# Nine of eleven feed-forward pairs as seven block products instead of seven, with normed operands from the second pair on

## The chip, the core and the metric

The kernel runs on one core of a Trainium2 chip. The core has engines with a queue each: TensorE for matmuls (PE in the profile; PEld is its weight load), VectorE (DVE), ScalarE (ACT), GpSimd (POOL) and SyncE (SP), which here only issues DMAs. On-chip data lies in 128 partitions; matmuls write to accumulators in PSUM, which VectorE and ScalarE read. The metric is the device time of one execution in microseconds (us); lower is better. Before the change the median of three runs is 1290.93 us.

## The reference

Two decoder layers on 512 tokens of width 1024 in float32. Each layer ends in a SwiGLU feed-forward and a gated embedding; only the feed-forward is touched:

```python
def rms_norm(x, g):
    xf = x.astype(jnp.float32)
    y = xf * lax.rsqrt(jnp.mean(xf * xf, axis=-1, keepdims=True) + EPS)
    return (y * g.astype(jnp.float32)).astype(x.dtype)

def swiglu(x, w_gate, w_up, w_down):
    return (jax.nn.silu(x @ w_gate) * (x @ w_up)) @ w_down
...
        u = rms_norm(h, ffn_norm_g[i])
        h = h + swiglu(u, ffn_w_gate[i], ffn_w_up[i], ffn_w_down[i])
```

The inner width is 2816, that is 22 blocks of 128.

## The kernel before

**Arithmetic.** Activations are kept transposed: a chunk is 128 features x 512 tokens, and the width of 1024 is eight chunks. Each float32 operand is split into an upper part (rounded by ScalarE) and the remainder (by VectorE). `mm3` (lines 161 to 165) makes one product of three matmuls, in this order: weight remainder by upper activation (163), upper weight by activation remainder (164), upper by upper (165).

**Feed-forward** (`ffn`, called once in each layer). The 22 blocks are taken two at a time, as eleven pairs, in three parts of 4, 4 and 3 pairs; after each part `linear` multiplies the hidden blocks by the down weights and adds them to `h`. `after.chunk` prepares the next norm.

A *direct* pair takes four weight tiles (gate and up of each block; `weight`, lines 146 to 159: a DMA on SyncE's queue into `wraw`, the upper part `whi` at 156, the remainder `wlo` at 158) and for each weight eight products with the chunks: 4 x 8 x 3 = 96 matmuls of 512 columns. The rows are `mm` in the profile.

The first pairs of a feed-forward (`RAW_PAIRS`) read raw chunks (`norm.u`, tiles `A`), which are not yet divided by the root mean square; the result is multiplied by the row `rb` (lines 745 and 747). `rb` is made from column sums (line 203), a diagonal matrix (227), a spreading matmul (237) and a copy by ScalarE (212). `normed` is a generator that `feed` advances: for each of the eight chunks it makes the normed chunk (592; tiles of the tags in `qtags`, and `wth` for the last two), its upper part (598) and its remainder (599), which later direct pairs read (`un`). After `uses[0] = None` it goes on to eight more steps: it makes differences of blocks of 256 columns of the normed chunks (618) and splits them (621, 622) into tiles `A`. `STEPS` says how many steps follow each half of a pair.

A pair *as seven products* (`strassen`) takes the gate weights of both blocks as a matrix of 2 x 2 blocks, and the up weights likewise, and forms each result from seven block products in place of eight, 7 x 4 x 3 = 84 matmuls of 256 columns each time. `operands` makes the combined weights: a tile of a tag in `qtags`, in the profile `C`, is loaded on SyncE's queue (649) and a second weight is added to it by an accumulating DMA on GpSimd's queue (650); a raw weight goes into `wraw` (652); sums with it are `wth` (666) and `wtl` (667); `split` makes upper parts and remainders (642, 643) in the ring of four `whi` and four `wlo`. The order of the products is 1 (which needs only `wraw`), 5 and 7 (the combined tile `C`), 2 and 6, 4, 3.

The tags of `SPACE` have two buffers at most, and the normed chunks lie in the same tags as the combined weights: in the first feed-forward chunks 0 to 3 in two buffers of `C5` and 4, 5 in `C4`; in the second 0, 1 in `C2`, 2, 3 in `C3` and 4, 5 in `C4`. The three tags are used in turn, beginning with the second of `qtags`.

**Order.** Each engine takes its queue in order. The program is written as above; a scheduler sets the order in each queue ahead of time, from its own model of times.

Before, the first two pairs of each feed-forward read raw chunks, the third and fourth normed ones, and the seven pairs of parts two and three are made of products.

Of the kernel before, what the change touches and what calls it, by code (L numbers as in the profile page):

```python
# [23 lines left out]
NC = D // P  # L24
# [57 lines left out]
    (("C5", "C5", "C4"), [(f"C{k // 2}",) for k in range(8)]),  # L82
    (("C2", "C3", "C4"), [(t,) for t in ("C0", "C0", "C1", "C1", "C5", "C5")] + [("D0", "D1"), ("D4", "D5")]),
)
RAW_PAIRS = 2
STEPS = (0, 2, 3, 3)
SEVEN = ((1,0),(1,1),(1,2),(1,3),(2,0),(2,1),(2,2))
QKV = (("q", 0, (0, 0, 0, 0)), ("v", 0, (0, 1, 1, 0)), ("q", 1, (1, 1, 2, 2)), ("q", 2, (0, 1, 2, 0)), ("v", 1, (1, 2, 2, 2)), ("q", 3, (0, 2, 0, 1)))


# [1 line left out]
def trunk(ctx, tc, xT, pT, wts, diag, dww, vec, rel, onehot, lamv, out):  # L92
# [9 lines left out]
    def sb(shape, tag, bufs, dt=F32):  # L102
        uid[0] += 1
        return pool.tile(shape, dt, tag=tag, name=f"{tag}_{uid[0]}", bufs=bufs)
# [40 lines left out]
    def weight(n=1024, pieces=1, between=(), eng=V, after=None):  # L145
        i = wnext[0]
        wnext[0] += 1
        raw = sb([P, 1024], "wraw", 2)
        hi = sb([P, 1024], "whi", 4, F32R)
        lo = sb([P, 1024], "wlo", 4, F32R)  # L150
        for k in range(pieces):
            cut = slice(k * n // pieces, (k + 1) * n // pieces)
            loaded[0] = nc.sync.dma_start(raw[:, cut], wts[i, :, cut])
            if k < len(between):
                between[k]()
            A.copy(hi[:, cut], raw[:, cut])  # L156
            with tc.issue_after(after.ins) if after else nullcontext():
                eng.tensor_tensor(lo[:, cut], raw[:, cut], f(hi[:, cut]), ALU.subtract)  # L158
        return hi, lo

    def mm3(acc, a, b, first, last):
        (ah, al), (bh, bl) = a, b
        T.matmul(acc, al, bh, start=first, stop=False)  # L163
        T.matmul(acc, ah, bl, start=False, stop=False)  # L164
        return T.matmul(acc, ah, bh, start=False, stop=last)  # L165

    def wpart(w, k):
        return tuple(t[:, k * P : (k + 1) * P] for t in w)
# [377 lines left out]
    def linear(n_in, src, consume, group0=1, before=None, after=None, first=(None,) * 3):  # L546


        m = 0
        while m < NC:  # L550
            g = group0 if m == 0 else 1
            ws = [weight(n_in * P, after=first[i] if m == 0 else None) for i in range(g)]
            accs = [mm() for _ in range(g)]
            for k in range(n_in):
                if before:
                    before(k)
                for w_, a_ in zip(ws, accs):
                    mm3(a_, wpart(w_, k), src[k], k == 0, k == n_in - 1)
                    if after:
                        after()  # L560
            for i in range(g):
                consume(m + i, accs[i])
            m += g
# [10 lines left out]
    def ffn(norm, after, space):  # L574
        qtags, utags = space
        rb = None
        un = []
        comb = {}
        uses = [None]
# [46 lines left out]
        making = [normed()]  # L626

        def feed(n=1):
            for _ in range(n):
                if making:  # L630
                    try:
                        next(making[0])
                    except StopIteration:
                        making.pop()
# [42 lines left out]
        def strassen(i):  # L677

            w = operands(i)

            def product(acc, name):
                for k in range(4):
                    mm3(acc, wpart(w[name], k), comb[name][k], k == 0, k == 3)

            one, two, three, four = sc(), mm(), mm(), tp()
            t, e, g = wk(), big(), big()
            first, second = slice(0, H2), slice(H2, S)
            product(one[:, first], 1)
            A.copy(t[:, first], one[:, first])
            A.mul(t[:, second], one[:, first], -1.0)  # L690
            product(three[:, first], 5)
            product(three[:, second], 7)
            product(two[:, first], 2)
            product(two[:, second], 6)
            V.tensor_tensor(e, two, t, ALU.add)
            V.tensor_tensor(
                g.rearrange("p (a s) -> p a s", a=2), three.rearrange("p (a s) -> p a s", a=2),
                e[:, second].unsqueeze(1).to_broadcast([P, 2, H2]), ALU.add,
            )
            V.tensor_tensor(e[:, second], three[:, second], g[:, first], ALU.add)  # L700
            product(four[:, second], 4)
            V.tensor_tensor(g[:, second], four[:, second], g[:, second], ALU.add)
            product(four[:, first], 3)
            V.tensor_tensor(g[:, first], four[:, first], g[:, first], ALU.subtract)
            return e, g

        seen = 0
        for at, (f0, n) in enumerate(PARTS):
            hid = []
            for pair in range(n // 2):  # L710
                hi, lo = (sb([P, 2, S], f"B{2 * pair + k}", 1, F32R) for k in range(2))
                for k in range(2):
                    hid.append((hi[:, k], lo[:, k]))
                if (at, pair) in SEVEN:
                    i = wnext[0]
                    wnext[0] += 4
                    gs = strassen(i)
                    for t in gs:
                        A.activation(t, t, AF.Silu)
                    us = strassen(i + 1)  # L720
                    for o, (t, g) in enumerate(zip(us, gs)):
                        V.tensor_tensor(t, t, g, ALU.mult)
                        first, step = (H2, H2) if o else (0, S + H2)
                        hs, ls = (bass.AP(x.tensor, x.offset + first, [list(x.ap[0]), [step, 2], [1, H2]]) for x in (hi, lo))
                        A.copy(hs, t.rearrange("p (a s) -> p a s", a=2))
                        V.tensor_tensor(ls, t.rearrange("p (a s) -> p a s", a=2), f(hs), ALU.subtract)
                    continue
                x = norm.u if seen < RAW_PAIRS else un
                for i in range(2):
                    wg, wu = weight(), weight()  # L730
                    pg, pu = mm(), mm()
                    for k in range(NC):
                        mm3(pg, wpart(wg, k), x[k], k == 0, k == NC - 1)
                    if rb is None:
                        norm.diagonal()
                    for k in range(NC):
                        mm3(pu, wpart(wu, k), x[k], k == 0, k == NC - 1)
                    if rb is None:
                        rb = norm.rows()
                    tg, tu = big(), big()  # L740
                    if x is un:
                        A.activation(tg, pg, AF.Silu)
                        V.tensor_tensor(tu, pu, tg, ALU.mult)
                    else:
                        V.tensor_tensor(tg, pg, rb, ALU.mult)
                        A.activation(tg, tg, AF.Silu)
                        V.tensor_tensor(tu, pu, rb, ALU.mult)
                        V.tensor_tensor(tu, tu, tg, ALU.mult)
                    A.copy(hi[:, i], tu)
                    V.tensor_tensor(lo[:, i], tu, f(hi[:, i]), ALU.subtract)  # L750
                    feed(STEPS[2 * seen + i] if 2 * seen + i < len(STEPS) else 2)
                seen += 1
                if seen == RAW_PAIRS:
                    assert len(un) == NC, len(un)
                    feed()
                    uses[0] = None

            def add(m, acc):
                V.tensor_tensor(h[m], acc, h[m], ALU.add)  # L759
                if at == len(PARTS) - 1:  # L760
                    after.chunk(m)

            linear(n, hid, add, 2)
# [28 lines left out]

    n2 = Norm("ple_g0")
    ffn(norm, n2, SPACE[0])
    norm = Norm("attn_g")
    ple(n2, pp, lambda m, cut: norm.chunk(m))
# [281 lines left out]
    linear(NC, ot, add_attn, 2, heads_until, step)  # L1078
    n2 = Norm("ple_g1")
    ffn(norm, n2, SPACE[1])  # L1080

    def store(m, cut):
# [130 lines left out]
```

## Time and profile before

| what | us |
|---|---|
| three runs | 1288.16, 1290.93, 1292.81 |
| the profiled execution | 1288.43 |
| its span in the profile | 1286.3 |
| busy: weight loads, VectorE, ScalarE, GpSimd | 1082.9, 886.0, 603.9, 268.4 |
| first feed-forward: part one's four pairs, its down projection | 219 to 308, 308 to 352 |
| second feed-forward: the same | 884 to 973, 973 to 1017 |

Times in the rows are counted from the start of the span. A row of the order of time gives start, duration, engine, line, operation, the tile written and those read, shapes, and in square brackets how long the engine had stood idle and which instruction ended that. "x3" is a count of like instructions, and the duration is then that of all. The page's slices of a fortieth of the span each:

```profile
PE   8999999999999999999999997999999999999998
DVE  6988647773478558766678887846953588558665
PEclk8999989999999999999999999999999999999999
```

A digit is the busy share in tenths, and in the last line the clock granted to TensorE.

### The profile page before, as it was taken

The numbers are of one execution on the slowest core, as the hardware profiler recorded it, in microseconds if no ns is written. First come the engines' busy times: TensorE is split into PE (matmuls) and PEld (weight loads), VectorE is DVE, ScalarE is ACT, GpSimd is POOL, SyncE is SP. The second block draws the span as 40 slices with busy tenths as digits, with TensorE's granted clock in tenths as the row PEclk, the third lists the DMA queues.
The fourth block names the chain that finished last, engine by engine and source line by source line (L and its number), as shares of the span: only waits on it lengthen the run. The fifth ranks groups of instructions, "written<-read, shape, count | busy, mean of one in ns | idle before, by whom it ended". The sixth has DMA issues, their size and how long they took to land. (4 is left out here: it accounts for less than half of the span.)

```text
span 1286.3 us, 18032 instructions
## 1 busy us (share of the span) xinstructions
PE 1253.5 (97%) x6912; PEld 1082.9 (84%) x6912; DVE 886.0 (69%) x1430; ACT 603.9 (47%) x999; POOL 268.4 (21%) x235
## 2 busy tenths in 40 slices
PE   8999999999999999999999997999999999999998
PEld 5888678888899989988888886778888899899887
DVE  6988647773478558766678887846953588558665
ACT  5642455442155325454566766734532255225442
POOL 4644323000000000033435534122000001000030
PEclk8999989999999999999999999999999999999999
DMA  6745314272456545243222221313463366444241
GB/s 228 226 154 167 116 49 116 81 213 82 115 155 174 148 123 134 69 127 104 80 87 92 83 64 50 98 49 116 119 175 99 105 172 175 136 113 117 81 137 66
DMA packets 58498, 154.15 MB, mean 120 GB/s; under 512 B 6275, under 2 KB 10883, under 8 KB 58412
## 3 DMA queue, kind: packets, MB, share of 16 engines
q1 hardware_dynamic: 52256, 134.89, 32.6%
q0 software_dynamic: 4032, 14.68, 6.9%
q10 hardware_dynamic: 2124, 3.43, 0.8%
q8 instruction: 54, 0.88, 0.3%
q14 instruction: 32, 0.26, 0.1%
HBM read 148.77 MB, written 4.21 MB: 119 GB/s over the span
## 5 line engine op out<-in xcount | busy, mean ns | idle before, releaser
L163 PE MATMUL mm<-A,wlo 128*128 128x512 f32 (+1 forms) x856 | 295.2, 350 | 5.6 <-ACT A L177 2.6
L164 PE MATMUL mm<-A,whi 128*128 128x512 f32 (+1 forms) x856 | 298.6, 350 | 0.3
L165 PE MATMUL mm<-A,whi 128*128 128x512 f32 (+1 forms) x856 | 296.5, 347 | 0.0
L156 ACT CAST whi<-wraw 128x1024 fp32r<-128x1024 f32 (+2 forms) x158 | 159.5, 1016 | 253.6 <-PE mm L165 120.0
L158 DVE TENSOR_TENSOR wlo<-wraw,whi 128x1024 fp32r<-128x1024 f32 (+2 forms) x154 | 196.3, 1278 | 86.3 <-ACT whi L156 86.1
L163 PEld LDWEIGHTS mm<-A,wlo 128*128 128x128 f32 x856 | 162.8, 190 | 28.5 <-DVE wlo L158 3.9
L164 PEld LDWEIGHTS mm<-A,whi 128*128 128x128 f32 x856 | 162.9, 190 | 24.2 <-DVE A L178 3.5
L165 PEld LDWEIGHTS mm<-A,whi 128*128 128x128 f32 x856 | 162.8, 190 | 20.6 <-issue 1.0
L164 PE MATMUL mm<-B,whi 128*128 128x512 f32 x352 | 137.2, 391 | 0.0
L165 PE MATMUL mm<-B,whi 128*128 128x512 f32 x352 | 137.1, 390 | 0.0
L163 PE MATMUL mm<-B,wlo 128*128 128x512 f32 x352 | 135.9, 392 | 0.0
L650 POOL DMA_DIRECT2D C<-in_wts x28 | 24.6, 878 | 520.0 <-DVE h L759 228.9
L197 POOL TENSOR_TENSOR acc<-acc,wk 128x512 f32<-128x512 f32 x42 | 66.1, 1574 | 229.2 <-ACT wk L196 121.2
L759 DVE TENSOR_TENSOR h<-mm,h 128x512 f32<-128x512 f32 x48 | 33.0, 688 | 75.2 <-PE mm L165 75.1
L165 PEld LDWEIGHTS mm<-B,whi 128*128 128x128 f32 x352 | 66.1, 188 | 14.5
L164 PEld LDWEIGHTS mm<-B,whi 128*128 128x128 f32 x352 | 66.1, 188 | 14.1
L163 PEld LDWEIGHTS mm<-B,wlo 128*128 128x128 f32 x352 | 66.1, 188 | 14.0
L165 PE MATMUL mm<-whi,A 128*128 128x512 f32 x192 | 75.7, 395 | 0.0
L164 PE MATMUL mm<-wlo,A 128*128 128x512 f32 x192 | 74.9, 395 | 0.0
L163 PE MATMUL mm<-whi,A 128*128 128x512 f32 x192 | 74.8, 396 | 0.0
L163 PE MATMUL mm<-C,wlo 128*128 128x512 f32 (+1 forms) x212 | 74.1, 350 | 0.0
L164 PE MATMUL mm<-C,whi 128*128 128x512 f32 (+1 forms) x212 | 73.8, 348 | 0.0
(269 smaller groups left out, 2593.8 us busy)
## 6 DMA issues: line engine op xcount, KB each, us to landing
wraw<-in_wts SPq DMA_DIRECT2D x166, 512.0 KB, 3.7
C<-in_wts SPq DMA_DIRECT2D x28, 512.0 KB, 4.5
C<-in_wts POOLq DMA_DIRECT2D x28, 512.0 KB, 6.0
bias<-in_wts SPq DMA_DIRECT2D x28, 256.0 KB, 3.6
wraw<-in_wts SPq DMA_DIRECT2D x16, 384.0 KB, 3.1
D<-in_diag SPq DMA_DIRECT2D x22, 256.0 KB, 4.8
C<-in_diag SPq DMA_DIRECT2D x16, 256.0 KB, 4.7
h<-in_xT SPq DMA_DIRECT2D x8, 256.0 KB, 5.8
```

Of the source, the lines that this page charges most:

```text
L156: A.copy(hi[:, cut], raw[:, cut])
L158: eng.tensor_tensor(lo[:, cut], raw[:, cut], f(hi[:, cut]), ALU.subtract)
L163: T.matmul(acc, al, bh, start=first, stop=False)
L164: T.matmul(acc, ah, bl, start=False, stop=False)
L165: return T.matmul(acc, ah, bh, start=False, stop=last)
L197: self.last = self.eng.tensor_tensor(self.acc, self.acc, sq, ALU.add)
L650: nc.gpsimd.dma_start(q, wts[i + 2].rearrange("p (a s) -> p a s", a=2), accum_op=ALU.add)
L759: V.tensor_tensor(h[m], acc, h[m], ALU.add)
```

## The change

Three constants and two loops change. `SEVEN` gains the third and fourth pair of part one, so that nine of eleven pairs of each feed-forward are made of products. Only the first pair reads raw chunks; the second reads normed ones. All eight normed chunks are fed in the first pair, all eight block differences in the second, and whatever is left is fed ahead of the first pair of products.

```diff
-RAW_PAIRS = 2
-STEPS = (0, 2, 3, 3)
-SEVEN = ((1,0),(1,1),(1,2),(1,3),(2,0),(2,1),(2,2))
+RAW_PAIRS = 1
+STEPS = (4, 5, 4, 5)
+SEVEN = ((0,2),(0,3),(1,0),(1,1),(1,2),(1,3),(2,0),(2,1),(2,2))
...
                 if (at, pair) in SEVEN:
+                    while making:
+                        feed()
                     i = wnext[0]
...
                 if seen == RAW_PAIRS:
-                    assert len(un) == NC, len(un)
-                    feed()
+                    while uses[0] is not un:
+                        feed()
                     uses[0] = None
```

Lines behind the added ones count two or four higher in the changed kernel. The orders of all engines change only in part one of each feed-forward, up to the start of its down projection. Three places:

TensorE, start of the second pair of the first feed-forward, before (the accumulator, then the chunk read and the weight; `A_304` is the first raw chunk, upper part, `A_305` its remainder):

```order
L165 MATMUL mm_1875<-A_344_1767,whi_1869 128x512
L163 MATMUL mm_1955<-A_304_1558,wlo_1945 128x512
L164 MATMUL mm_1955<-A_305_1559,whi_1944 128x512
L165 MATMUL mm_1955<-A_304_1558,whi_1944 128x512
L163 MATMUL mm_1955<-A_306_1564,wlo_1945 128x512
L164 MATMUL mm_1955<-A_307_1565,whi_1944 128x512
```

and in the changed kernel (`C_367` holds both parts of the first normed chunk, `C_368` of the second):

```order
L165 MATMUL mm_1893<-A_344_1767,whi_1887 128x512
L163 MATMUL mm_1983<-C_367_1864,wlo_1973 128x512
L163 MATMUL mm_1984<-C_367_1864,wlo_1979 128x512
L163 MATMUL mm_2079<-C_367_1864,wlo_2069 128x512
L164 MATMUL mm_1983<-C_367_1864,whi_1972 128x512
L165 MATMUL mm_1983<-C_367_1864,whi_1972 128x512
L163 MATMUL mm_1983<-C_368_1868,wlo_1973 128x512
L164 MATMUL mm_1984<-C_367_1864,whi_1978 128x512
```

The second pair now reads normed chunks, and three of its groups are interleaved, chunk by chunk, where one group ran through at a time.

SyncE's queue, part one of the second feed-forward, before (`C_1798`, `C_1776` and `C_1756` are the combined tiles of the third, second and first set of products, `wraw` raw weights):

```order
L649 DMA C_1798_9397<-in_wts 128x2x512
L153 DMA wraw_8634<-in_wts 128x1024
L649 DMA C_1776_9262<-in_wts 128x2x512
L153 DMA wraw_8711<-in_wts 128x1024
L153 DMA wraw_8717<-in_wts 128x1024
L649 DMA C_1756_9133<-in_wts 128x2x512
L153 DMA wraw_8794<-in_wts 128x1024
```

and after (`C_1762`, `C_1740`, `C_1720` the third, second and first set's; `C_1782` the fourth's):

```order
L652 DMA wraw_8848<-in_wts 128x1024
L652 DMA wraw_8977<-in_wts 128x1024
L649 DMA C_1762_9109<-in_wts 128x2x512
L649 DMA C_1740_8974<-in_wts 128x2x512
L649 DMA C_1720_8845<-in_wts 128x2x512
L652 DMA wraw_9112<-in_wts 128x1024
L649 DMA C_1782_9238<-in_wts 128x2x512
```

The order among the three tiles is the same, third, second, first; the weights of two direct pairs that stood between and behind them are gone, and the raw weights of the products stand there.

VectorE, second feed-forward, after: the end of the second pair and of the block differences (`wk`), up to the remainder for products 5 and 7 (`wlo_8857`). The last difference that reads chunks 2 and 3, whose buffer `C_1720` takes, stands seven rows ahead of the first row here:

```order
L752 TENSOR_TENSOR B_1673_8650<-big_8714,B_1672_8649 128x512
L622 TENSOR_TENSOR A_1717_8840<-wk_8836,A_1716_8839 128x512
L666 TENSOR_TENSOR wth_8860<-C_1720_8845,wraw_8848 128x512
L666 TENSOR_TENSOR wth_8989<-C_1740_8974,wraw_8977 128x512
L667 TENSOR_TENSOR wtl_8861<-wth_8860,wraw_8848 128x512
L745 TENSOR_TENSOR big_8810<-mm_8760,big_8809 128x512
L643 TENSOR_TENSOR wlo_8857<-C_1720_8845,whi_8856 128x1024
```

Before, the first of these sums (666) stood in the down projection that follows part one:

```order
L158 TENSOR_TENSOR wlo_9069<-wraw_9067,whi_9068 128x1024
L666 TENSOR_TENSOR wth_9148<-C_1756_9133,wraw_9136 128x512
L759 TENSOR_TENSOR h_10_89<-mm_8977,h_10_89 128x512
L667 TENSOR_TENSOR wtl_9149<-wth_9148,wraw_9136 128x512
L158 TENSOR_TENSOR wlo_9101<-wraw_9099,whi_9100 128x1024
```

So the sums with the combined tile moved from the down projection to the end of the second pair, right behind the block differences.

## The prediction

> **What bounds the kernel now.** I read the page's busy times first, then the table of stretches, then the order of time on single engines around the places that the change touches.
>
> ```profile
> span 1286.3 us, 18032 instructions
> PE 1253.5 (97%) x6912; PEld 1082.9 (84%) x6912; DVE 886.0 (69%) x1430; ACT 603.9 (47%) x999; POOL 268.4 (21%) x235
> ```
>
> TensorE is busy for 97% of the span, so two things count: how long its matmuls take, and where a new wait stops it. The table of stretches has, after the limits, the length and each engine's busy time with its instruction count, the granted clock, the DMA share and GB/s.
>
> ```profile
> 243.00:264.60 21.60, 21.60 (x97) 17.88 (x96) 21.60 (x35) 11.18 (x17) 1.05 (x1) 1.00 0.41 138
> 243.20:351.80 108.60, 108.60 (x479) 89.53 (x478) 63.12 (x91) 34.85 (x47) 3.68 (x4) 1.00 0.45 129
> 371.00:391.00 20.00, 20.00 (x169) 20.00 (x168) 17.65 (x29) 11.01 (x18) 1.74 (x2) 1.00 0.67 177
> 478.40:537.00 58.60, 58.60 (x489) 58.48 (x488) 44.86 (x69) 30.87 (x50) 1.74 (x2) 1.00 0.37 100
> ```
>
> Row one is the second pair of the first feed-forward: VectorE is busy for all of it, making normed operands and block sums. Row two is direct work alone (matmuls of 512 columns), row four product work alone (256 columns). In row three, one pair as products, VectorE has 17.65 of 20.00 us to do: it cannot catch up by much there.
>
> **What the pairs save.** Counts include one or two matmuls that reach over an edge, so I use 478 and 487. Direct: 108.60/478 = 0.227 us from start to start; a pair has 96, 21.8 us. Products: 58.60/487 = 0.120 us; a pair has 2 x 7 x 12 = 168, 20.2 us. That is 1.6 us a pair, and with four more pairs **-6.4 us**. The weight loads are why it isn't an eighth of 21.8: PEld is busy for 58.48 of 58.60 us in row four.
>
> The Trainium skill, page "TensorE: Matmul & The Clock Gate", section "Back-to-back issue gap", gives N/2.4 + 2.5 ns. By that, as an estimate, 512 columns take 216 ns and 256 take 109, a pair would save 2.4 us and the four 9.5, and the sum below would come out 3.1 us lower. The rows show 227 and 120 ns, so they decide.
>
> **The first new wait: operands of the second pair.** The diagonal matrix and its spreading matmul stand where they stood; VectorE starts when the row `rb` arrives. In order of time (start, duration, engine, line), VectorE and then TensorE:
>
> ```profile
> 237.74 0.69 DVE L745 TENSOR_TENSOR big<-mm,rb 128x512 f32<-128x512 f32 x1 [3.20 <-ACT rb L212]
> 239.54 4.05 DVE L592 SCALAR_TENSOR_TENSOR C<-h,vec,rb 128x512 f32<-128x512 f32 x6
> 243.52 1.41 DVE L592 SCALAR_TENSOR_TENSOR wth<-h,vec,rb 128x512 f32<-128x512 f32 x2
> 244.84 1.21 DVE L158 TENSOR_TENSOR wlo<-wraw,whi 128x1024 fp32r<-128x1024 f32 x1
> 245.98 0.68 DVE L748 TENSOR_TENSOR big<-big,big 128x512 f32<-128x512 f32 x1
> 246.58 0.75 DVE L618 TENSOR_TENSOR wk<-C 128x256 f32<-128x256 f32 x2
> 247.25 1.88 DVE L599 TENSOR_TENSOR C<-C,C 128x512 fp32r<-128x512 f32 x3
> 249.06 0.68 DVE L747 TENSOR_TENSOR big<-mm,rb 128x512 f32<-128x512 f32 x1
> ...
> 912.59 1.89 DVE L599 TENSOR_TENSOR C<-C,C 128x512 fp32r<-128x512 f32 x3
> ```
>
> ```profile
> 242.86 0.39 PE L163 MATMUL mm<-A,wlo 128*128 128x512 f32 x1
> ...
> 908.20 0.39 PE L163 MATMUL mm<-A,wlo 128*128 128x512 f32 x1
> ```
>
> Now the second pair reads the normed chunks and not the raw ones. In the order of the changed kernel VectorE has the same work up to the first lower half (line 599), which in these rows ends at 247.25 + 0.68 = 247.9. TensorE reaches the second pair at 242.86 and may start three matmuls, which read upper halves; the fourth, due at 243.54, needs that lower half. So it waits 247.9 - 243.5 = **4.4 us**; behind it nothing else can pass. In the second feed-forward the same rows give 913.27 - 908.88 = 4.4 us. After it no chunk is late: each serves three interleaved groups, 9 x 0.227 = 2.0 us, and VectorE writes a lower half every 0.60 us (1.88 for three, 249.06 - 247.25). The pair ends at 247.9 + 93 x 0.227 = 269.1.
>
> **The second new wait: combined weights of the third pair.** Each set of products loads a tile `C` by SyncE's queue, then adds to it by a DMA of GpSimd's queue (lines 649, 650). The buffer is free only when the block sums (line 618) have read the normed chunks in it. Before, that was hidden behind two pairs and the down projection; now the tile is wanted at once. The rows of SyncE's and GpSimd's queue, and the time to landing of all such transfers around each:
>
> ```profile
> 258.23 0.38 SPq L649 DMA_DIRECT2D C<-in_wts  x1
> 263.43 1.05 POOL L650 DMA_DIRECT2D C<-in_wts  x1 [32.83 <-ACT A L621]
> C<-in_wts POOLq DMA_DIRECT2D x3, 512.0 KB, 8.8
> wraw<-in_wts SPq DMA_DIRECT2D x7, 512.0 KB, 5.4
> ...
> 936.05 0.74 DVE L618 TENSOR_TENSOR wk<-C,wk 128x256 f32<-128x256 f32 x2
> 936.88 0.38 SPq L649 DMA_DIRECT2D C<-in_wts  x1
> 942.33 0.86 POOL L650 DMA_DIRECT2D C<-in_wts  x1 [9.08 <-DVE big L743]
> C<-in_wts POOLq DMA_DIRECT2D x3, 512.0 KB, 6.9
> ...
> wraw<-in_wts SPq DMA_DIRECT2D x166, 512.0 KB, 3.7
> ```
>
> The load starts 0.1 us after the last sum that reads the old content (936.05 + 0.74, 936.88): so the buffer is what it waits for. From there to landing it is 5.2 + 8.8 = 14.0 us in the first feed-forward, 5.45 + 6.9 = 12.35 in the second.
>
> First feed-forward. I add up VectorE's order from 247.25 with 0.60 us for each row of 512, 0.67 for two of 256 (247.25 - 246.58), 1.14 for each weight remainder of 1024 (245.98 - 244.84). Up to the end of the last sum on chunks 0 and 1 stand eight lower halves, four more rows of 512, four of 256 and one weight: 12 x 0.60 + 1.34 + 1.14 = 9.7, which gives 257.0. The tile lands at 257.1 + 14.0 = **271.1**. ScalarE's upper half and VectorE's lower half follow:
>
> ```profile
> L642 ACT CAST whi<-C 128x1024 fp32r<-128x1024 f32 x28 | 29.3, 1047 | 32.4 <-PE mm L165 20.7 <-PE tp L165 11.7
> ```
>
> 1.05 + 1.14 puts products 5 and 7 at 273.3. TensorE is through product 1 at 269.1 + 1.4 = 270.5: **2.8 us**. Then a raw weight: the first set's raw tile `wraw` is read until 5.2 us after the landing (276.3: the remainder, three more rows of 512 and two sums follow the cast), the third set's is loaded into it in 4.5 us (between the 5.4 here and the 3.7 of the whole program), to 280.9, and two sums on it stand in VectorE's list ahead of the second set's first remainder: 1.2 + 1.14, so the second set starts at 283.3. TensorE, with products 5, 7, 2, 6 and 4 from 273.3 on, is there at 273.3 + 60 x 0.120 = 280.5: **2.8 us**. For later sets the same addition leaves VectorE about 1 to 5 us ahead.
>
> Second feed-forward. Its tags differ, and the order on SyncE's and GpSimd's queues has the tile of the third set first, then the second, then the first, which takes the buffer of chunks 2 and 3. That is free after the sums on those, 5.7 us further down VectorE's list than 257.0, so 262.7 + 665.3 = 928.0 (665.3 is 908.20 - 242.86). Landing: 928.1 + 12.35 = **940.4**. Four rows of 512 and the remainder, 2.4 + 1.14, precede product 5: 944.0. TensorE is there at 270.5 + 665.3 = 935.8: **8.2 us**. The next raw weight is asked for 1.8 us after the landing and comes in time.
>
> **The clock.** A long wait also costs speed afterwards:
>
> ```profile
> 84.70:88.10 3.40, 1.52 (x13) 1.41 (x13) 3.33 (x6) 0.00 (x0) 0.00 (x0) 1.00 0.62 193
> 88.10:91.50 3.40, 3.40 (x18) 3.40 (x18) 3.33 (x5) 2.91 (x5) 1.33 (x2) 0.50 0.32 66
> ```
>
> After a stretch of 3.4 us with TensorE busy for 1.52 of it, the next 3.4 us are granted 0.50. A half-speed stretch full of matmuls loses 1.7 us. After a 4.4 us wait that only shortens the wait that follows in the same feed-forward; after the 8.2 us it adds **1.7 us**. The Trainium skill's same page, section "What's actually happening", has the half clock after one idle window of about 3.4 us; the trace agrees in the length and is harsher in the condition (1.52 us of work did not save it).
>
> **Sum.** -6.4 + (4.4 + 2.8 + 2.8) + (4.4 + 8.2 + 1.7) = +17.9 us. The profiled execution took 1288.4 us (span 1286.3 and 2.1 around it): **1306.3 us**. The median of the runs, 1290.9, lies 2.5 above it, so a sum on the median would be 1308.8. Nothing behind each first down projection moves: there the orders are the same.
>
> What the trace doesn't show is how long these DMAs take when three such tiles are asked for within 6 us. Single landings before went from 5.4 to 9.1 us:
>
> ```profile
> DMA to landing us min/median/max: 5.4/6.5/9.1
> ```
>
> With 5.4 the tile's waits shrink to 0 and 2.2 (first) and 6.7 us (second): 1301. With 9.1 they grow to 3.1, 2.8 and 10.4: 1309. I stay with the medians of the two places, since they are of the same two queues at the same two places. Without the clock's term or with it at each wait: 2 less, 3 more.
>
> **Rivals.**
> - *The loads don't wait for the sums* (a second buffer of the tag is free). Then only 2 x 4.4 remains: -6.4 + 8.8 = +2.4, 1290.8, within 0.3%. Against it: 936.05 + 0.74 and 936.88 above.
> - *VectorE has a lead*, the faster side. Place: where `rb` arrives, before line 745 at 237.74. All four waits shrink with every microsecond that it comes earlier; the sum is zero with a lead of about 9 us (1.0 us is left in the first feed-forward, 3.6 and the clock's 1.7 in the second, against 6.4), and with 13 us all is saved: 1282.0. For it: VectorE idles 3.20 us just ahead. Against it: a lead of 9 us means 228.7, and the column sums that `rb` is made of are only then multiplied (line 203, last fence).
> - *More wait than the walk*: landings at 9.1, half clock at every wait, and VectorE, at 17.65 of 20.00, carries its lateness into the down projection: 1309 + 3 + 1 = 1313.
>
> ```profile
> 228.58 0.73 PE L203 MATMUL tp<-ones,acc 128*128 128x1 f32 x6
> ```
>
> **How the numbers follow.** Forecast 0.73, loads free 0.10, lead 0.04, more wait 0.13. A difference of 0.3% (3.9 us) is about what a measurement of this kernel can tell from none: faster 0.04, same 0.11 (loads free and a little of the forecast's low end), slower 0.85. The range from 1297 to 1313 holds the forecast with its bounds and most of the last rival, and leaves out 0.17.
>
> **What would show it.** In the changed profile: 3024 against 2352 product matmuls at 0.120 us; TensorE idle for some 4.4 us at 243 and 913, released by VectorE's line 599; idle again near 271, 281 and, longest, 936, released by the lower half of `C`; after the last a granted clock of 0.5 for a stretch. No idle at 936 makes the second wait wrong, none at 243 the first; a product pair at 19.5 us or less makes the saving wrong.

## The result and the profile after

The changed kernel takes 1311.03 us (median of four runs, 1308.24 to 1313.99), the kernel before, run beside it, 1291.57: a ratio of 1.015, 95% interval 1.0126 to 1.0174. It is 19.5 us slower by the medians and 22.7 by the profiled executions (1311.1 against 1288.43). The forecast was 17.9 slower: 1306.3 for the profiled execution, 1308.8 on the median. From the page of the changed kernel, the lines that answer to those of before:

```profile
span 1309.3 us, 18764 instructions
PE 1258.5 (96%) x7200; PEld 1099.5 (84%) x7200; DVE 926.3 (71%) x1502; ACT 624.5 (48%) x1039; POOL 275.3 (21%) x243
PEclk8999989999999999999999998899989999999999
```

TensorE has 288 more matmuls (4 pairs x (168 - 96)) and should be busy for 6.4 us less, yet it is busy for 5.0 us more: some of them ran at half clock. The other 18 us that the span has grown by are pauses. The waits of TensorE from 236 to 320 us and from 908 to 1000 us (the row waited in, what ended it, us in total, times, longest):

```profile
PE mm L163 <- DVE wlo L158: 2.6, 1, 2.6
PE sc L163 <- DVE wlo L643: 2.1, 1, 2.1
PE mm L164 <- DVE C L599: 1.4, 1, 1.4
...
PE mm L163 <- DVE wlo L643: 7.3, 1, 7.3
PE mm L163 <- DVE wlo L158: 2.6, 1, 2.6
PE mm L164 <- DVE C L599: 1.4, 1, 1.4
```

In the kernel before, neither window has a wait in this view. The table of stretches, first for the kernel before, from the first matmul of the first feed-forward to the last of its first down projection:

```profile
219.30:351.90 132.60, 132.60 (x586) 109.18 (x585) 78.06 (x111) 45.11 (x62) 6.88 (x6) 1.00 0.41 118
```

and in the changed kernel between the same two matmuls, then in the second feed-forward (132.6 before as well), four stretches behind waits, and product work alone:

```profile
220.60:360.10 139.50, 133.37 (x731) 116.10 (x730) 97.41 (x147) 55.09 (x82) 10.40 (x10) 0.98 0.51 135
892.80:1038.60 145.80, 134.51 (x731) 117.25 (x730) 97.28 (x147) 56.03 (x83) 10.19 (x10) 0.95 0.50 129
...
249.10:252.50 3.40, 3.22 (x8) 2.54 (x9) 3.40 (x8) 0.34 (x2) 0.00 (x0) 0.50 0.29 113
283.26:286.66 3.40, 3.40 (x18) 3.40 (x17) 3.37 (x6) 0.66 (x2) 0.00 (x0) 0.50 0.83 230
921.50:924.90 3.40, 3.40 (x9) 2.66 (x10) 3.40 (x7) 0.45 (x1) 0.00 (x0) 0.51 0.23 93
949.00:959.20 10.20, 6.12 (x29) 6.12 (x30) 7.93 (x12) 4.25 (x8) 0.78 (x1) 0.51 0.45 129
...
484.00:524.00 40.00, 40.00 (x330) 39.77 (x329) 29.52 (x45) 19.85 (x32) 1.75 (x2) 1.00 0.53 133
```

So part one costs 6.9 us more in the first feed-forward and 13.2 more in the second, and behind each of the waits stands a stretch with a granted clock of 0.5; in the kernel before part one has 1.00 throughout. The last row gives 40.00/330 = 0.121 us for a product matmul, as before.

**The first wait**, in order of time, VectorE and then TensorE:

```profile
246.14 1.21 DVE L158 TENSOR_TENSOR wlo<-wraw,whi 128x1024 fp32r<-128x1024 f32 x1
248.54 1.88 DVE L599 TENSOR_TENSOR C<-C,C 128x512 fp32r<-128x512 f32 x3
...
244.16 0.61 PE L163 MATMUL mm<-C,wlo 128*128 128x512 f32 x2
247.40 0.50 PE L163 MATMUL mm<-C,wlo 128*128 128x512 f32 x1 [2.63 <-DVE wlo L158]
249.28 0.79 PE L164 MATMUL mm<-C,whi 128*128 128x512 f32 x1 [1.37 <-DVE C L599]
```

TensorE pauses twice: for the weight remainder of the third interleaved group, and then for the lower half of the first chunk. With three starts at 0.227 us the fourth was due at 244.84; it came at 249.28, 4.4 us late.

**The combined tile**, first feed-forward (VectorE's last sum on the old content, SyncE's load, GpSimd's accumulating DMA, ScalarE's upper half), and in the second feed-forward the third of the three accumulating DMAs, VectorE and TensorE:

```profile
257.57 0.75 DVE L618 TENSOR_TENSOR wk<-C,wk 128x256 f32<-128x256 f32 x2
258.39 14.47 SPq L649 DMA_DIRECT2D C<-in_wts  x4
262.92 1.06 POOL L650 DMA_DIRECT2D C<-in_wts  x1 [31.02 <-DVE A L622]
268.92 1.05 ACT L642 CAST whi<-C 128x1024 fp32r<-128x1024 f32 x1 [4.25 <-DMA C<-in_wts]
...
943.47 0.86 POOL L650 DMA_DIRECT2D C<-in_wts  x1 [4.93 <-DMA C<-in_wts]
949.40 1.29 DVE L666 TENSOR_TENSOR wth<-C,wraw 128x512 f32<-128x512 f32 x2 [8.45 <-DMA C<-in_wts]
953.08 0.58 PE L163 MATMUL mm<-A,wlo 128*128 128x256 f32 x1 [7.28 <-DVE wlo L643]
```

The load starts 0.07 us after the sum that frees its buffer (257.57 + 0.75 = 258.32). In the first feed-forward the tile is there 6.0 us after GpSimd's issue, before TensorE asks for it at about 273: no wait. In the second, three such chains stand one behind the other, and everything down to TensorE idles for the last.

### The profile page after: what moved, and what is told of

Its sections match the earlier page's. It is cut to its first block, busy times and chain, and to the rows that moved or that the text cites. A ratio compares the mean times of both kernels' runs of the same rounds, so it can differ in the third digit from the quotient of the medians.

```text
span 1309.3 us, 18764 instructions
## 1 busy us (share of the span) xinstructions
PE 1258.5 (96%) x7200; PEld 1099.5 (84%) x7200; DVE 926.3 (71%) x1502; ACT 624.5 (48%) x1039; POOL 275.3 (21%) x243
## 5 line engine op out<-in xcount | busy, mean ns | idle before, releaser
L163 PE MATMUL mm<-A,wlo 128*128 128x256 f32 (+1 forms) x888 | 299.0, 342 | 11.9 <-DVE wlo L643 7.7
L164 PE MATMUL mm<-A,whi 128*128 128x256 f32 (+1 forms) x888 | 302.6, 342 | 2.2 <-DVE A L178 1.8
L165 PE MATMUL mm<-A,whi 128*128 128x256 f32 (+1 forms) x888 | 299.6, 338 | 0.0
L156 ACT CAST whi<-wraw 128x1024 fp32r<-128x1024 f32 (+2 forms) x142 | 142.7, 1012 | 222.0 <-PE mm L165 92.2
L158 DVE TENSOR_TENSOR wlo<-wraw,whi 128x1024 fp32r<-128x1024 f32 (+2 forms) x138 | 178.0, 1292 | 64.5 <-ACT whi L156 64.3
L163 PEld LDWEIGHTS mm<-A,wlo 128*128 128x128 f32 x888 | 170.4, 192 | 32.4 <-DVE wlo L643 7.5
L164 PEld LDWEIGHTS mm<-A,whi 128*128 128x128 f32 x888 | 170.5, 192 | 24.6 <-DVE A L178 6.0
L165 PEld LDWEIGHTS mm<-A,whi 128*128 128x128 f32 x888 | 170.6, 192 | 17.9 <-issue 1.0
L650 POOL DMA_DIRECT2D C<-in_wts x36 | 31.6, 878 | 533.8 <-DVE h L761 181.1
L222 POOL TENSOR_TENSOR r<-v,mhalf 128x8 f32<-128x8 f32 (+1 forms) x31 | 46.6, 1503 | 115.7 <-DVE v L220 93.4
L643 DVE TENSOR_TENSOR wlo<-wraw,whi 128x1024 fp32r<-128x1024 f32 x36 | 44.0, 1223 | 31.2 <-ACT whi L642 31.0
```

The source lines that it names most:

```text
L222: last_pow[0] = G.tensor_tensor(r[:, :n], v[:, :n], mhalf[:, :n], ALU.pow)
L643: V.tensor_tensor(lo, raw, f(hi), ALU.subtract)
L650: nc.gpsimd.dma_start(q, wts[i + 2].rearrange("p (a s) -> p a s", a=2), accum_op=ALU.add)
```

## The experiments

Each table value of the two feed-forwards is the time between the same two matmuls as in the rows above; "outside" is all other time up to the last matmul. These three columns are of one profiled execution each. That of the kernel before took 3.1 us less than its median, those of e3_own and e7_own_early 3.9 and 3.4 more, so 2 or 3 us outside say little. Each ratio is to the kernel before as run beside that kernel; its medians there went from 1289.54 to 1292.47.

| kernel | us (median) | ratio to before, 95% | first ff | second ff | outside |
|---|---|---|---|---|---|
| before | 1291.57 | | 132.6 | 132.6 | 1016.1 |
| changed | 1311.03 | 1.0126 to 1.0174 | 139.5 | 145.8 | 1019.0 |
| e1_raw2 | 1313.76 | 1.0160 to 1.0194 | 139.8 | 147.1 | 1019.5 |
| e2_eight | 1284.22 | 0.9936 to 0.9960 | 131.1 | 131.1 | 1014.9 |
| e10_eight_raw1 | 1299.12 | 1.0034 to 1.0081 | 138.4 | 137.2 | 1017.6 |
| e3_own | 1302.81 | 1.0058 to 1.0100 | 136.9 | 136.1 | 1027.0 |
| e6_early | 1299.84 | 1.0031 to 1.0083 | 132.9 | 142.3 | 1019.6 |
| e7_own_early | 1290.95 | 0.9985 to 1.0015 | 131.8 | 133.0 | 1022.8 |
| e9_held | 1291.19 | 0.9991 to 1.0024 | 130.1 | 132.1 | 1024.1 |
| e11_held | 1286.50 | 0.9932 to 0.9968 | 131.8 | 130.0 | 1018.8 |
| e12_raw2_held | 1295.03 | 1.0009 to 1.0037 | 133.8 | 133.8 | 1020.7 |

**Two raw pairs again, nine pairs of products.** This takes the first wait away and keeps the demand for the combined tile.

```diff
-RAW_PAIRS = 1
-STEPS = (4, 5, 4, 5)
+RAW_PAIRS = 2
+STEPS = (0, 2, 3, 3)
```

> Nine of eleven pairs stay products, but the first two pairs read raw chunks again, as before. Theory (the end of part one is set by VectorE's list and by the combined tiles, which wait for the block sums in it, so waits at the two places do not add): the 4.4 us wait and the half clock at the second pair go, TensorE comes to the third pair 6 us earlier and waits there some 6 to 10 us longer; the time is within 5 us of the changed kernel, 1306 to 1316 us. Rival (the wait at the second pair is a price of its own, 4.4 + 1.7 us in each feed-forward): 12 us below the changed kernel, about 1299 us.

TensorE's waits in the same two windows of e1_raw2:

```profile
PE mm L163 <- DVE wlo L643: 6.9, 2, 4.9
PE tp L163 <- DVE big L702: 0.9, 1, 0.9
...
PE mm L163 <- DVE wlo L643: 15.8, 1, 15.8
```

The wait at the second pair is gone. In the second feed-forward TensorE therefore stands at products 5 and 7 of the third pair 6.0 us earlier than in the changed kernel (939.8 against 945.8), and what it needs there comes 2.5 us later (955.6 against 953.1): 15.8 us of wait in one piece, with 17 us at half clock around it. In the first the waits come to 7.8 us. 1313.76 us, not better than the change. The early normed operands are not the fault by themselves; what the third pair needs has to be ready a pair earlier in either case.

**Eight pairs, the third direct.** As e1_raw2, and `SEVEN` without `(0,2)`; only one pair is added to the products.

```diff
-STEPS = (4, 5, 4, 5)
-SEVEN = ((0,2),(0,3),...
+STEPS = (0, 2, 3, 3, 4, 4)
+SEVEN = ((0,3),...
```

> Eight of eleven pairs as products (only the fourth pair of part one is added), raw chunks in two pairs, a direct third pair on normed chunks, under which the block sums and the combined tiles can be made. Theory (the products do save 1.6 us a pair, and only the hand-off costs): no wait over 1 us in part one, two pairs saved, 3.2 us less than before: about 1288 us, ratio 0.9975. Rival (a pair of products in part one costs more than it saves whatever stands ahead of it): over 1295 us.

No wait of TensorE is left in either window. Each part one is 1.5 us shorter than before (132.6 to 131.1): one pair's saving alone, as predicted. This kernel beats both, at a ratio of 0.9948. That is more than the 0.9975 that was expected: the two parts account for 3.0 us of some 7, and the rest isn't explained.

**Eight pairs with one raw pair.** The change with its third pair direct: the first wait alone.

```diff
-STEPS = (4, 5, 4, 5)
-SEVEN = ((0,2),(0,3),...
+STEPS = (4, 5, 2, 2, 2, 3)
+SEVEN = ((0,3),...
```

> One raw pair as in the changed kernel, but eight pairs of products, the third pair direct as before, and the block differences fed over the second and third pair: the first wait alone, with no combined tile wanted early. Theory: two pairs saved, -3.2 us, and in each feed-forward a wait of 4.4 us at the start of the second pair with one half-clock stretch behind it (1.6 us): +12, in all +9, 1300, ratio 1.007; no wait at products 5 and 7. Rival (a wait at the second pair is absorbed because what follows waits in any case): no more than 1292, ratio 1.0.

The waits, the same rows in both windows:

```profile
PE mm L163 <- DVE wlo L158: 2.6, 1, 2.6
PE mm L164 <- DVE C L599: 1.4, 1, 1.4
```

and nothing else. In the second feed-forward -1.6 + 4.4 + 1.7 (one stretch at half clock) = +4.5, measured +4.6; in the first, with two such stretches, +5.8. 1299.12 us lies on the theory's 1300, and above the 1292 that the rival allowed. Between e2_eight and this kernel, ratios of 0.9948 and 1.0058, stands the price of the first wait with its clock: 13.4 us within the two feed-forwards.

**Buffers of their own for the normed chunks.** The changed kernel, with the six chunks in three tags that are idle there, so that the combined tiles need not wait for the sums.

```diff
-                        two = sb([P, 2, S], qtags[c // 2], 2)
+                        two = sb([P, 2, S], ("B6", "B7", "B5")[c // 2], 1)
```

> The changed kernel, with the first six normed chunks in buffers of the hidden tiles of the third and fourth pair, so that the combined tiles needn't wait for the block sums. Theory (the buffer is what the tile waits for): the 7.6 us wait in the second feed-forward and its 10 us of half clock go, about 10 us, and most of the 2.4 us in the first with its 1.7; the two waits at the second pair stay, 4.4 us each with 1.7 of half clock. About 1297 to 1299 us. Rival (VectorE's list is late in itself, the tile only comes last): 1307 us or more.

The waits for line 643 are gone in both feed-forwards; the 2.6 and 1.4 at the second pair stay (2.6 and 1.1 in the second). The second feed-forward falls from 145.8 to 136.1. That is the shared buffer's price, shown. In the first feed-forward only 2.6 us are saved, and the first wait leaves 6.8 us at half clock there. The median, 1302.81, lies between the theory's 1299 and the rival's 1307, for 8 us are lost outside (in the profiled execution, the slowest of its four): with the buffers free so early, the loads of the first combined tiles moved into the layer norm that precedes the feed-forward, more on which below.

**`rb` earlier.** The changed kernel, with the spreading matmul ahead of nearly all matmuls of the first pair's second block.

```diff
-            A.copy(r, spread(self.dg))
+            t = tp()
+            self.spread = T.matmul(t, ones, self.dg, start=True, stop=True)
+            A.copy(r, t)
...
                     for k in range(NC):
-                        mm3(pu, wpart(wu, k), x[k], k == 0, k == NC - 1)
+                        with tc.issue_after(norm.spread.ins) if late else nullcontext():
+                            mm3(pu, wpart(wu, k), x[k], k == 0, k == NC - 1)
```

> The changed kernel, with the spreading matmul that makes rb in the first pair placed ahead of the matmuls of that pair's second block, in each feed-forward, and nothing else moved. Theory (waits of one feed-forward share VectorE's list and the combined tile, so what is taken off the first is partly handed on): rb comes about 3.3 us earlier, the first wait falls from 4.45 to about 1.1 us and leaves no half-clock stretch; the chunk sums end 3.3 us earlier too, but TensorE arrives 4.4 to 5 us earlier at products 5 and 7, so the tile's wait in the second feed-forward grows from 7.6 to about 9 us and the raw weight's in the first from 2.4 to about 4. Changed kernel less 5 to 7 us: 1304 to 1306, ratio to before 1.010. Rival (each wait stands for itself): both first waits and their clock go, 2 x (3.3 + 1.6), and the second waits stay or shrink: 1299 to 1301, ratio 1.006.

TensorE's column sums and the spreading matmul in e6_early:

```profile
232.18 0.73 PE L203 MATMUL tp<-ones,acc 128*128 128x1 f32 x6
236.05 1.02 PE L213 MATMUL tp<-wk,ones 128*128 128x512 f32 x2
```

These stand 3.9 us apart; in the changed kernel 7.5 (229.87 and 237.36), so `rb` comes 3.6 us earlier. The waits:

```profile
PE tp L163 <- DVE wlo L645: 1.3, 1, 1.3
PE mm L163 <- DVE wlo L645: 1.1, 3, 0.6
...
PE mm L163 <- DVE wlo L645: 9.9, 1, 9.9
```

In the second feed-forward the theory holds: 4.4 us and a half-clock stretch are saved ahead of the tile, and the tile's wait grows from 7.3 to 9.9, so only 3.5 of the 6.1 us remain. In the first it does not: the waits that are left come to 2.4 us in four pieces, not to 4 and more, and 6.6 us are saved. The tile is in time there with the earlier demand too, so nothing is handed on to it. But that the raw weight's wait did not grow may have a reason that is neither theory's: VectorE's order is another there. In the changed kernel (first two rows) the second set's first remainder stands behind the third set's sum, which waits for the raw weight; in e6_early (last two) it stands ahead of it.

```profile
280.33 0.69 DVE L666 TENSOR_TENSOR wth<-C,wraw 128x512 f32<-128x512 f32 x1 [1.96 <-DMA wraw<-in_wts]
281.67 1.22 DVE L643 TENSOR_TENSOR wlo<-wraw,whi 128x1024 fp32r<-128x1024 f32 x1
...
276.27 1.22 DVE L645 TENSOR_TENSOR wlo<-wraw,whi 128x1024 fp32r<-128x1024 f32 x1
281.09 0.69 DVE L668 TENSOR_TENSOR wth<-C,wraw 128x512 f32<-128x512 f32 x1 [1.86 <-DMA wraw<-in_wts]
```

So the time, 1299.84, is the rival's, but the first feed-forward doesn't decide between the two theories.

**Both together.** e3_own's line and e6_early's.

> As the kernel with buffers of their own, and the spreading matmul for the row rb is put ahead of the second block's matmuls of the first pair, where its diagonal is ready, so rb should come some 3.5 to 4 us earlier. Theory: the wait at the second pair shrinks from 4.4 to about 1 us and is too short for the clock to drop; with four pairs saved at 1.6 us (6.4) and 2 to 4 us of waits left, about 2 to 4 us below before: 1287 to 1289 us, ratio 0.997 to 0.999. Rival (VectorE has too much to do in the first three pairs for any order): over 1297 us.

Both kinds of wait are gone up to rests of 1.3 and 0.5 us (first) and 1.8 us (second feed-forward), and the two parts one are down to 131.8 and 133.0. Yet the kernel only draws even, 1290.95, above the theory's 1289 and below the rival's 1297: in the profiled execution 6.7 us more than before are outside. Rows of the queues of SyncE and GpSimd in e7_own_early:

```profile
143.67 2.38 SPq L651 DMA_DIRECT2D C<-in_wts  x2
150.42 1.05 POOL L652 DMA_DIRECT2D C<-in_wts  x1
```

In the changed kernel the first of these loads stands at 258.39.

**The loads held back, by an instruction of another engine.**

```diff
+            with tc.issue_after(norm.spread.ins) if turn[0] < 4 else nullcontext():
                 nc.sync.dma_start(q, bass.AP(...
                 nc.gpsimd.dma_start(q, wts[i + 2]...
```

> The kernel of e7_own_early, with the loads of the first three combined tiles of each feed-forward held until the spreading matmul that makes rb has been issued; before that they were issued in the layer-norm region some 60 us earlier, where the 20 us up to 180 us were granted a clock of 0.56 and the start of the feed-forward came 7 to 8 us later. Theory: those loads cost the 7 to 8 us there; held, the start of the first feed-forward is back at 220 to 221 us, the tiles still land before they are wanted, and the residual waits (1.6, 0.8 and 2.1 us) stay: e7's 1290.95 less 5 to 8 us, 1283 to 1286, ratio to before 0.994 to 0.996. Rival: the delay in the layer-norm region comes from the freed buffers in another way (another order of the conv's work), and the time stays at 1289 to 1292, ratio 1.0.

The edit did not do what it was made for: the loads still go out at 140.57 and 149.97 us. The spreading matmul is TensorE's, and asking for an order behind it did not move the loads of SyncE and GpSimd. It tells nothing between the theories, and repeats e7_own_early (1291.19).

**The loads held back on their own queues.** SyncE's behind the load of the first block's second weight, GpSimd's behind the reciprocal root that `rb` comes from.

```diff
+                        begun[:] = loaded[0], last_pow[0]
...
+            with tc.issue_after(begun[0].ins) if turn[0] < 4 else nullcontext():
                 nc.sync.dma_start(q, bass.AP(...
+            with tc.issue_after(begun[1].ins) if turn[0] < 4 else nullcontext():
                 nc.gpsimd.dma_start(q, wts[i + 2]...
```

> In e9_held the loads of the combined tiles still went out at 140 and 150 us: an order against an instruction of another engine had not moved them. Here they are ordered behind instructions of their own queues: SyncE's load behind the first pair's weights, GpSimd's accumulating DMA behind the reciprocal root that rb is made of; else the kernel is e7_own_early. Theory (the early loads cost the 6 to 8 us in the layer-norm region): the start of the first feed-forward is back at 220 to 222 us, 140:160 has a DMA share near 0.2 again instead of 0.6 to 0.8, the residual waits of 3 to 4 us stay: 1283 to 1286, ratio to before 0.994 to 0.997. Rival (the delay comes of the freed buffers' other effects on the order there): 1289 to 1292, ratio 1.0.

The stretches around the layer norm, e7_own_early and then e11_held:

```profile
140.00:160.00 20.00, 16.84 (x87) 11.93 (x85) 14.65 (x19) 6.20 (x10) 13.33 (x11) 0.99 0.66 164
160.00:180.00 20.00, 18.62 (x61) 14.53 (x62) 7.09 (x15) 7.27 (x15) 4.62 (x4) 0.59 0.16 52
```

```profile
140.00:160.00 20.00, 18.07 (x89) 12.55 (x88) 17.84 (x24) 7.31 (x12) 11.43 (x9) 1.00 0.19 65
160.00:180.00 20.00, 18.56 (x75) 13.74 (x76) 10.51 (x17) 12.06 (x22) 7.29 (x6) 0.83 0.18 51
```

With the loads held, the DMA share of the first stretch falls from 0.66 to 0.19, VectorE does 17.84 us of work there in place of 14.65, the granted clock of the second rises from 0.59 to 0.83, and the first feed-forward starts at 220.7 us and not at 227.3. What the early loads delay can be seen at four loads of 64 KB on SyncE's queue (line 367) that VectorE waits for in this place. They are issued at 151.22 and land after 6.1 us in e7_own_early (5.9 in e9_held, 5.8 in e3_own); in e11_held they are issued at 152.14 and land after 2.1 (2.0 in the changed kernel):

```profile
159.09 1.09 DVE L372 SCALAR_TENSOR_TENSOR B<-B,vec,shrow 128x512 f32<-128x512 f32 x1 [4.78 <-DMA B<-po]
155.79 1.12 DVE L372 SCALAR_TENSOR_TENSOR B<-B,vec,shrow 128x512 f32<-128x512 f32 x1 [1.34 <-DMA B<-po]
```

The theory holds: ratio 0.995, inside its range (1286.50 us is half a microsecond above it), and the early loads are enough to explain the delay of e3_own and e7_own_early. This is the change with its waits taken out. Its second feed-forward, with 0.3 us of wait left, is 2.6 us shorter than before; two pairs at 1.6 us less the 0.6 that this pause takes from start to start make 2.6.

**The same with two raw pairs.** e11_held with the `RAW_PAIRS` and `STEPS` of e1_raw2.

> As e11_held, but with two raw pairs and normed chunks and block differences made as before the change, and still nine pairs of products. Theory (the waits come of VectorE's list being asked for a pair early and of the shared buffers; neither is left at the second pair, and the third pair's operands have 21 us more): what remains is a wait at the third pair of no more than 3 us in each feed-forward, against 6.4 us saved: 1284 to 1290, ratio 0.995 to 0.999. Rival (VectorE has 17.65 of 20.00 us of work in a pair of products and cannot make the block differences and sums before the third pair): waits of 5 us and more at products 5 and 7 as with two raw pairs alone, 1295 or above, ratio 1.004 or above.

The waits, the same in both feed-forwards:

```profile
PE mm L163 <- DVE wlo L645: 2.8, 1, 2.8
```

The wait is within the theory's 3 us, the time (1295.03) is the rival's. In each part one -3.2 + 2.8 + 1.7 for a half-clock stretch = +1.3, measured +1.2. The rest lies outside. Against e11_held 1.7 us of it are lost ahead of the first feed-forward, in the layer norm again, where no early load stands now, and 2.0 behind the second part one; between the two, 1.8 are gained. The layer norm:

```profile
140.00:160.00 20.00, 16.16 (x57) 10.18 (x56) 17.62 (x23) 9.07 (x16) 11.39 (x9) 0.91 0.13 47
160.00:180.00 20.00, 19.55 (x64) 14.39 (x65) 7.44 (x14) 8.35 (x16) 7.28 (x6) 0.66 0.12 29
```

TensorE pauses there for 3.2 us against 1.7 in e11_held, and the granted clock falls to 0.66. So this place can lose time without early loads too; what makes that pause longer was not tried.

## Why the prediction was right, and where it was off

**What the pairs save: right.** 1.6 us a pair: 1.5 for one pair in e2_eight, 2.6 plus a rest of 0.6 for two in e11_held.

**The first new wait: right in place and size**, 4.4 us in both feed-forwards, and e10_eight_raw1 shows it alone. The working named only the lower half (line 599). The trace has a weight remainder ahead of it as the end of 2.6 of the 4.0 us; both stand in VectorE's list behind `rb`, so the sum is the same.

**The second wait, second feed-forward: right.** 8.2 forecast, 7.3 idle by the waits' view (7.6 from start to start). The landing was put at 940.4; 8.0 us later all round, since the pair begins at 916.2 and not at 908.2, that is 948.4, against 949.4 when VectorE resumes: 13.2 us behind the load's start and not 12.35.

**The second wait, first feed-forward: the tile's 2.8 us was mis-sized.** The load began as the walk had it: 257.1 moved by the 1.3 us that the second pair began later is 258.4, measured 258.39. But the step "From there to landing it is 5.2 + 8.8 = 14.0 us" was taken from a place where other loads ran, and here it was 10.5 (258.39 to 268.92). One weight was loaded between 255 and 275 us, where it was five before; that this is the reason is likely but not shown by itself. The prediction had an end at 5.4 for this term and gave 0 for the wait there; that end is what happened. The raw weight's wait was 2.1 (2.4 from start to start) of 2.8 forecast.

**The clock: the step that failed most.** The forecast priced one half-clock stretch, 1.7 us behind the tile's wait in the second feed-forward. That wait left three (949.00 to 959.20, 6.12 us of work at 0.51, 3.1 us lost). In the first feed-forward the raw weight's wait of 2.1 us was followed by one too (283.26, 1.7 us lost), though the text priced no clock there. "After a 4.4 us wait that only shortens the wait that follows in the same feed-forward" held in the second, where the tile's wait followed. In the first no wait came at products 5 and 7, so the next was the raw weight's. Whether that would have been longer without the 1.6 us lost at 249.10 was not tried; the raw weight and VectorE's rows, which end it, hang on the tile's landing there. The Trainium skill, page "TensorE: Matmul & The Clock Gate", section "What's actually happening", asks for an idle window of about 3.4 us before the half clock. The pause ahead of 283.26 was 2.4 us long with matmuls on both sides, so the runs are harsher than the Trainium skill.

**The sum.** By feed-forward the forecast was -3.2 + 4.4 + 2.8 + 2.8 = +6.8 and -3.2 + 4.4 + 8.2 + 1.7 = +11.1; measured are +6.9 and +13.2. The first is right by luck: 2.8 for the tile that did not come and 0.4 too much for the raw weight, against two half-clock stretches (1.6 + 1.7) that were left out. In the second, what the tile's wait ends on came 1.0 us later than forecast and the clock behind it cost 1.4 more, which is about the 2.1. The 2.9 us left of the profiles' difference lie outside the two parts: 1.3 ahead of the first feed-forward, whose first matmul starts at 220.6 and not at 219.3, and the rest behind the second part one. Both kernels have the same orders in these places. The kernels without early loads range from 1014.9 to 1020.7 us outside, so a single profile doesn't tell whether the change caused these 2.9; this stays open.

**The rivals.** That the loads don't wait for the sums is ruled out by the 0.07 us at 258.32, and by e3_own, in which the waits for the tile are gone. The lead of VectorE: "All four waits shrink with every microsecond" was wrong; e6_early has the lead, 3.6 us, and the tile's wait in the second feed-forward grew. While the first wait lasts, a lead brings TensorE to the tile as much earlier as the tile itself. Of the third rival, more wait than the walk, the half clock at every wait is what happened; the landings after 9.1 us did not, they took 5.9.

## What to carry to other kernels

A cheaper form of a matmul stage pays only if its operands can be ready a stage earlier: count what the helper engine must finish between the last input and the first use, and find whose buffer each new load waits for, before counting matmuls. As an estimate from these runs, price a pause of TensorE of 2 us and more at its length plus 1.7 us for every stretch of 3.4 us full of matmuls that it leaves at half clock, unless another wait swallows them. And when a buffer is freed to let a load start early, say on the load's own queue how early it may go: here the early loads took back the 6 us that the change without its waits saves (ratios of 1.000 and 0.995).

## What was not expected of the hardware

- How long the half clock lasts. Behind pauses of 2.1 (e7_own_early, second feed-forward), 2.4 and 4.4 us it held for 3.4 us (6.8 in e10_eight_raw1's first feed-forward and in both of e3_own); with one of 7.6 us for 10.2, with 10.2 us (e6_early) for 13.7, and with 16 us (e1_raw2) for 17, in these three from within the pause on. Pauses of up to 1.9 us (e9_held, second feed-forward) left none, and neither did one of 2.3 in e1_raw2's first, so the length alone doesn't decide.
- An accumulating DMA of 512 KB on GpSimd's queue landed in 8.8 us before, where many weights were being loaded beside it, and in 5.9 us at the same place now. The three that stand there now, and the loads around them, by the profile's list of issues from 255 to 275 us in the changed kernel:

```profile
C<-in_wts SPq DMA_DIRECT2D x4, 512.0 KB, 4.2
C<-in_wts POOLq DMA_DIRECT2D x3, 512.0 KB, 5.9
wraw<-in_wts SPq DMA_DIRECT2D x1, 512.0 KB, 5.4
```

One weight is loaded in these 20 us now; in the same 20 us before it was five.
